# Reading the moving operand of fp32r products alternately from two halves of its block

## The chip, the cores and the metric

The kernel runs on one core of a Trainium2 chip. The metric is the device time of one execution in microseconds; the figure for the kernel before is the median of three runs. The profile comes from one more execution, and its span reaches from the first to the last instruction. The weights are permuted on the host before the launch; that is not part of the time.

## The reference

One layer of a hybrid encoder over 256 tokens with 2048 features, all in fp32. Cut to its products:

```python
mod = c_act @ ada_w + ada_b                     # 2048 x 12288: shift, scale, gate for two sub-layers
h = rms_norm(x, norm_mix_w) * (1 + scale_m) + shift_m
proj = h @ w_in                                 # q, k, v, o, z, conv inputs, gates, merge gates
h_a = bidirectional(mlstm_chunkwise, ...)       # 4 heads
y_a = (sigmoid(a_o) * rms_norm(h_a)) @ w_branch_a
qkv = silu(centred_depthwise_conv(b_qkv, gdn_conv_w))
o_b = bidirectional(gated_delta_chunkwise, ...) # 16 heads
y_b = (rms_norm(o_b) * silu(b_z)) @ w_branch_b
x = x + gate_m * ((g_a * y_a + g_b * y_b) @ w_out)
hf = rms_norm(x, norm_ffn_w) * (1 + scale_f) + shift_f
gt, up = split(hf @ w_gate_up)                  # 2048 x 11264
x = x + gate_f * ((silu(gt) * up) @ w_down)     # 5632 x 2048
return rms_norm(x, norm_final_w)
```

The change concerns all weight products except the modulation and the first sixteen column blocks of the input projection.

## The kernel before

**Split products.** A weight product is computed from fp32r operands, in three parts. Each operand is a high part (its rounding to fp32r) plus a low part (the remainder): `hh` and `hl` for the tokens, `wh` and `wl` for the weights. The product is high x high + low x high + high x low, added up in PSUM. TensorE takes a stationary operand of 128 x 128, loaded by an instruction of its own, and streams a moving operand of up to 512 columns past it.

**Two forms of product.** A product *by feature* (`fjob`, line 173) takes a block of 128 output features. The weight block `wh[:, k]` (128 x 128) is stationary and the tokens `hh[:, kk]` (256 columns) are the moving operand, in lines 187 to 189. The result has features on the partitions and tokens along the row. A product *by token* (`tjob`, line 195) takes 512 output features. The tokens `xh[:, kk, c]` (128 of them) are stationary and 512 weight columns are the moving operand, in lines 230 to 232; the result has tokens on the partitions. Where a product has `by_token`, its last chunk runs for one token block after the other (lines 253 to 255).

**Weights on their way.** The weights of one step come as a 1 MB block, issued by SyncE into one of three `raw` buffers. ScalarE copies half a block into `wh` (line 209 by token, 182 by feature), and VectorE subtracts to get `wl` (line 211 or 184). `wh` and `wl` have three buffers each; a buffer comes free when the last product that reads it is done. A block by token feeds 24 products. On the host, `_groups` (line 1449) and the array `gu` (line 1507) lay the weights out so that a block of 4 x 128 rows by 512 columns is one contiguous piece.

**Evictions.** A finished product by feature is copied out of PSUM by ScalarE: into a padded buffer for the convolution (`gdn_conv`, line 329, the `b` products) or into a buffer that goes to memory (`keep_f`, line 358, the `a` products). Products by token are read out by ScalarE or VectorE in `done` functions, in the order of their columns. There are four accumulators of one PSUM bank each (`acc_ps`).

**Order of the work.** The first part (line 557) works with full-precision fp32 products. Then the heads of the gated delta rule run between the projection products, which fill TensorE while the heads' short steps wait for each other (`fill`, `stream`). The mLSTM heads follow, then the branch and output projections. The feed-forward layer alternates a gate and an up product for each of eleven blocks of 512 features, then runs the down product in four groups of columns. Modulation sums on VectorE are spread over all of this (`pump`, `ada_parts`). The head steps include one in which 64 lanes invert 32 x 32 triangles by shrinking column loops (lines 692 and 698, on VectorE), the mLSTM's denominators (line 950), and the scores of a head (line 630), which are full-precision fp32 products.

Of the kernel before, what the change touches and what calls it, by code (L numbers as in the profile page):

```python
# [11 lines left out]
AF = mybir.ActivationFunctionType  # L12
# [3 lines left out]
P = 128  # L16
T = 256
D = 2048
KB = D // P
# [33 lines left out]
def hybrid_block(ctx: ExitStack, tc: tile.TileContext, xr, nfr, crow, pk_d, cst_d, ada2, ada4, win0, winb, wint, wba, wbb, wo, wgu, wd, out, dbg=None):  # L53
    nc = tc.nc
    V, S, G, PE = nc.vector, nc.scalar, nc.gpsimd, nc.tensor
# [12 lines left out]
    def big(p, dt, name):  # L68
        return p.tile([P, KB, T], dt, tag="b16", name=name)

    def order(ins, yes=True):

        return tc.keep_in_program_order(ins) if yes else ins
# [62 lines left out]
    def raw_tile(shape, name):  # L136

        since[0] += 1
        if since[0] > 2 and asked and room[0][0] is st:
            add()  # L140
        return st.tile(shape, F32, tag="raw", bufs=3, name=name)
# [4 lines left out]
    def settle(keep=0, only=None):  # L146

        now = [f for f in behind if only is None or f.__name__ == only]
        for f in now[: len(now) - keep]:
            behind.remove(f)  # L150
            f()
# [13 lines left out]
    def pump():  # L165
        count[0] += 1
        if every[0] and count[0] % every[0] == 0:
            owed[0] += 1
        if owed[0] and not held[0]:
            owed[0] -= 1  # L170
            sums()

    def fjob(name, src, done):

        ps = acc_ps.tile([P, 512], F32, tag="acc", name=f"acc_{name}")
        o = ps[:, :T]
        raw = raw_tile([P, KB, P], f"raw_{name}")
        nc.sync.dma_start(raw, src)
        for k0 in range(0, KB, 8):
            wh = st.tile([P, 8, P], F32R, tag="wh", bufs=3, name=f"wh_{name}_{k0}")  # L180
            wl = st.tile([P, 8, P], F32R, tag="wl", bufs=3, name=f"wl_{name}_{k0}")
            S.activation(wh, raw[:, k0 : k0 + 8], AF.Copy)
            settle()
            V.tensor_tensor(wl, raw[:, k0 : k0 + 8], wh.bitcast(F32), ALU.subtract)
            for k in range(8):
                kk = k0 + k
                PE.matmul(o, wh[:, k], hh[:, kk], start=kk == 0, stop=False)  # L187
                PE.matmul(o, wh[:, k], hl[:, kk], start=False, stop=False)  # L188
                PE.matmul(o, wl[:, k], hh[:, kk], start=False, stop=kk == KB - 1)  # L189
            if k0:  # L190
                pump()
                done(o)
            yield True

    def tjob(name, chunks, xh, xl, done, early=0, by_token=None, steps=1, parts=((0, slice(0, 512)), (1, slice(0, 512)))):

        raws = {}

        def halves(u, k0):
            if u not in raws:
                raws[u] = raw_tile([P, 4, 512], f"raw_{name}_{u}")
                nc.sync.dma_start(raws[u], chunks[u])
            wh = st.tile([P, 2, 512], F32R, tag="wh", bufs=3, name=f"wh_{name}_{u}_{k0}")
            wl = st.tile([P, 2, 512], F32R, tag="wl", bufs=3, name=f"wl_{name}_{u}_{k0}")
            order(S.activation(wh, raws[u][:, k0 : k0 + 2], AF.Copy), early)  # L209
            settle()  # L210
            order(V.tensor_tensor(wl, raws[u][:, k0 : k0 + 2], wh.bitcast(F32), ALU.subtract), early)  # L211
            return wh, wl

        todo = [(u, k0) for u in range(len(chunks)) for k0 in (0, 2)]
        made = []
        for i, q in enumerate(todo[:early]):
            made.append(halves(*q))
            if steps > 1 or i == early - 1:
                yield True
        ps = [acc_ps.tile([P, 512], F32, tag="acc", name=f"acc_{name}_{t}") for t in range(2)]  # L220
        last = 4 * len(chunks) - 1
        if by_token:
            todo = todo[:-2]
        for n, (u, k0) in enumerate(todo):
            wh, wl = made.pop(0) if made else halves(u, k0)
            for k in range(2):
                kk = 4 * u + k0 + k
                for t in range(2):
                    c = slice(t * P, (t + 1) * P)
                    order(PE.matmul(ps[t], xh[:, kk, c], wh[:, k], start=kk == 0, stop=False), early and steps > 1)  # L230
                    PE.matmul(ps[t], xl[:, kk, c], wh[:, k], start=False, stop=False)  # L231
                    PE.matmul(ps[t], xh[:, kk, c], wl[:, k], start=False, stop=kk == last)  # L232
            if k0:
                pump()
                if u == len(chunks) - 1:
                    done(ps)
            yield True
            if early and steps > 1:
                if n + early < len(todo):
                    made.append(halves(*todo[n + early]))  # L240
                yield True
        if by_token:
            w = [halves(len(chunks) - 1, k0) for k0 in (0, 2)]
            by_token()
            for i, (t, part) in enumerate(parts):
                if i > 1:
                    ps.append(acc_ps.tile([P, 512], F32, tag="acc", name=f"acc_{name}_{i}"))
                c = slice(t * P, (t + 1) * P)
                o = ps[i][:, : part.stop - part.start]
                for k in range(4):  # L250
                    kk = last - 3 + k
                    wh, wl = (a[:, k % 2, part] for a in w[k // 2])
                    PE.matmul(o, xh[:, kk, c], wh, start=i == 2 and not k, stop=False)
                    PE.matmul(o, xl[:, kk, c], wh, start=False, stop=False)
                    PE.matmul(o, xh[:, kk, c], wl, start=False, stop=kk == last)
                done(t, ps[i], part)
                yield True
# [34 lines left out]
    hh = big(bigA, F32R, "hh")  # L292
    hl = big(bigA, F32R, "hl")
# [9 lines left out]
    for i in range(NP_):  # L303
        pd = fr.tile([P, T + 4], F32, name=f"pad{i}")
# [5 lines left out]
    def decay_load(h):  # L310
        al = als[h] = fr.tile([P, 2, T + 8], F32, tag="al", bufs=2, name=f"al{h}")
        order(G.memset(al[:, :, 0:8], 0.0))
        order(G.dma_start(al[:, :, 8:], alpha_d[:, h].partition_broadcast(P)))

    def gdn_conv(h, j, ps):

        if j == 0:
            kq = fr.tile([P, 2, T], F32, tag="kq", bufs=2, name=f"kq{h}")
            vf = fr.tile([P, T], F32, tag="vf", bufs=2, name=f"vf{h}")
            parts[h] = (kq, vf)  # L320
            if h == 1:
                decay_load(h)
        kq, vf = parts[h]
        cb = (16 + h, h, 32 + h)[j]
        w = [pk[:, PK_CONV + 5 * cb + i : PK_CONV + 5 * cb + i + 1] for i in range(5)]
        pd = pads[npad[0] % NP_]
        npad[0] += 1
        if ps is not None:
            S.activation(pd[:, 2 : T + 2], ps, AF.Copy)
        settle(1)  # L330
        cv = fr.tile([P, T], F32, tag="cv", bufs=2, name=f"cv{h}_{j}")
        S.activation(cv, pd[:, 2 : T + 2], AF.Copy, scale=w[2])
        for i in (0, 1, 3, 4):
            V.scalar_tensor_tensor(cv, pd[:, i : i + T], w[i], cv, ALU.mult, ALU.add)

        def end():
            order(S.activation(kq[:, j] if j < 2 else vf, cv, AF.Silu))
            if ps is None:
                evict(3 * h + j + 1 + NP_)

        behind.append(end)
# [13 lines left out]
    def keep_f(dst, name):  # L355
        def done(ps):
            ev = evp.tile([P, T], F32, tag="evf", bufs=2, name=f"ev_{name}")
            S.activation(ev, ps, AF.Copy)
            S.dma_start(dst, ev)
        return done  # L360

# [29 lines left out]
    def evict(o):  # L391

        if o <= 3 * GRP:
            S.activation(pads[(o - 1) % NP_][:, 2 : T + 2], first[o], AF.Copy)
# [597 lines left out]
    last = (0, 1, 2, 1, 2, 2, 1, 1, 3, 0)  # L992
# [433 lines left out]
    for g in range(4):  # L1426
        c = slice(g * 512, (g + 1) * 512)
# [18 lines left out]
    return np.ascontiguousarray(w.reshape(kb, P, nb, P).transpose(2, 1, 0, 3))  # L1446


def _groups(w):
    k, n = w.shape  # L1450
    return np.ascontiguousarray(w.reshape(k // 512, 4, P, n // 512, 512).transpose(3, 0, 2, 1, 4))


def _fm(v):
# [3 lines left out]
def _arrays(x, c, ada_w, ada_b, norm_mix_w, w_in, mlstm_b_i, mlstm_b_f, mlstm_norm_w, gdn_conv_w,  # L1458
# [26 lines left out]
    w = w_in[0]  # L1485
# [5 lines left out]
    for h in range(NH_A):  # L1491
# [15 lines left out]
    gu = w_gate_up[0].reshape(4, 4, P, 2, KD, 512).transpose(4, 3, 0, 2, 1, 5)  # L1507
# [9 lines left out]
        "winb": np.ascontiguousarray(win[13:]),  # L1517
        "wint": wint,
        "wba": _groups(w_branch_a[0]),
        "wbb": _groups(w_branch_b[0]),  # L1520
        "wo": _groups(w_out[0]),
        "wgu": np.ascontiguousarray(gu),
        "wd": _groups(w_down[0]),
    }

# [16 lines left out]
```

## Time and profile before

| | us |
|---|---|
| runs: median (lowest to highest of 3) | 2053.01 (2051.42 to 2057.70) |
| the profiled execution: span | 2054.3 |
| TensorE with a product under way | 2017.2 |
| VectorE busy | 1397.7 |
| ScalarE busy | 1027.4 |
| mean granted TensorE clock | 0.992 |

In the profile, PE is the products on TensorE, PEld the loads of stationary operands (which run beside the products), DVE is VectorE, ACT ScalarE, POOL GpSimd and SP SyncE. A group's row gives the line of the kernel, the engine, the operation, the tile written and the tiles read, the shape and the count, then the busy time in us and the mean duration of one in ns, then the idle time before and what ended it. A product's duration counts from its start to the end of its drain, and the next product starts earlier than that.

### The profile page before, as it was taken

To read this page: it belongs to the slowest core of one execution; us is meant where nothing else is said; L and a number is where in the kernel's file an instruction comes from. 1 tells how busy PE (TensorE), PEld (TensorE's weight loads), DVE (VectorE), ACT (ScalarE), POOL (GpSimd) and SP (SyncE) were. 2 spreads that over 40 slices of the span, in tenths; PEclk is the share of its full clock that TensorE was granted. 3 is DMA by queue.
4 is the path that set the end of the run, shared out by engine and by line. 5 is a ranking of instruction groups with operands and counts; after the bars stand their busy time and mean duration, and the time that the engine had idled before them with its cause. 6 is when DMAs were issued, how large, how long until landed. Compare 5 with 4: busy or idle time off the path is not lost.

```text
span 2054.3 us, 27025 instructions
## 1 busy us (share of the span) xinstructions
PE 2017.2 (98%) x10386; PEld 1698.6 (83%) x10386; DVE 1397.7 (68%) x2062; ACT 1027.4 (50%) x1541; POOL 116.6 (6%) x211
## 2 busy tenths in 40 slices
PE   8999999999999999999999999999999999999998
PEld 6878789988997888889787888788888888878886
DVE  5778877877888788866577778756556554555554
ACT  3146647765675667455534444644444444444443
POOL 0001210111011010100100000200000000000000
PEclk9999999999999999999999999999999999999999
DMA  9986666656666666686776877466666665555553
GB/s 400 420 332 209 195 224 227 220 165 212 226 199 221 245 205 226 205 288 260 260 269 254 309 292 289 163 236 237 237 226 234 254 226 187 193 194 196 193 192 136
DMA packets 78962, 485.64 MB, mean 236 GB/s; under 512 B 10585, under 2 KB 15969, under 8 KB 24433
## 3 DMA queue, kind: packets, MB, share of 16 engines
q1 hardware_dynamic: 63216, 450.69, 60.5%
q0 software_dynamic: 8160, 17.88, 3.9%
q10 hardware_dynamic: 7458, 15.36, 2.0%
q8 instruction: 81, 1.33, 0.3%
q14 instruction: 47, 0.39, 0.1%
HBM read 467.07 MB, written 16.82 MB: 236 GB/s over the span
## 4 chain that ended last, share of the span: by engine, by line
PE 86%; DMA 6%; DVE 5%; ACT 1%; issue 1%; POOL 0%; ACTq 0%; SPq 0%; DVEq 0%; POOLq 0%
PE acc_gt L230 4%; PE acc_gt L232 4%; PE acc_gt L231 4%; PE acc_up L232 4%; PE acc_up L231 4%; PE acc_up L230 4%; PE acc_d L230 4%; PE acc_d L232 4%; PE acc_d L231 4%; DMA ra<-ada 3%; PE acc_o L232 3%; PE acc_o L230 3%; PE acc_o L231 3%; PE acc_b L187 2%; PE acc_b L188 2%; PE acc_b L189 2%
## 5 line engine op out<-in xcount | busy, mean ns | idle before, releaser
L211 DVE TENSOR_TENSOR wl_d<-raw_d,wh_d 128x1024 fp32r<-128x1024 f32 x88 | 107.9, 1226 | 119.9 <-ACT wh_d L209 119.9
L211 DVE TENSOR_TENSOR wl_up<-raw_up,wh_up 128x1024 fp32r<-128x1024 f32 x88 | 107.8, 1226 | 111.9 <-ACT wh_up L209 111.9
L211 DVE TENSOR_TENSOR wl_gt<-raw_gt,wh_gt 128x1024 fp32r<-128x1024 f32 x88 | 108.6, 1234 | 89.1 <-ACT wh_gt L209 89.1
L187 PE MATMUL acc_b<-hh,wh_b 128*128 128x256 f32 x576 | 164.7, 286 | 0.0
L209 ACT ACTIVATE wh_d<-raw_d 128x1024 fp32r<-128x1024 f32 x88 | 93.3, 1061 | 139.0 <-PE acc_d L231 134.0
L189 PE MATMUL acc_b<-hh,wl_b 128*128 128x256 f32 x576 | 160.8, 279 | 0.0
L188 PE MATMUL acc_b<-hl,wh_b 128*128 128x256 f32 x576 | 159.6, 277 | 0.0
L209 ACT ACTIVATE wh_gt<-raw_gt 128x1024 fp32r<-128x1024 f32 x88 | 93.3, 1060 | 128.7 <-PE acc_gt L231 77.3
L111 DVE SCALAR_TENSOR_TENSOR ada<-ada,crow 128x2048 f32<-128x2048 f32 x64 | 146.2, 2284 | 10.8 <-DMA ada<-ada 10.8
L209 ACT ACTIVATE wh_up<-raw_up 128x1024 fp32r<-128x1024 f32 x88 | 93.2, 1060 | 118.0 <-PE acc_up L231 84.2
L230 PE MATMUL acc_gt<-wh_gt,hfh 128*128 128x512 f32 x352 | 139.2, 395 | 0.1
L231 PE MATMUL acc_gt<-wh_gt,hfl 128*128 128x512 f32 x352 | 138.3, 393 | 0.0
L232 PE MATMUL acc_gt<-wl_gt,hfh 128*128 128x512 f32 x352 | 137.5, 391 | 0.0
L230 PE MATMUL acc_up<-wh_up,hfh 128*128 128x512 f32 x352 | 136.9, 389 | 0.0
L231 PE MATMUL acc_up<-wh_up,hfl 128*128 128x512 f32 x352 | 136.9, 389 | 0.0
L232 PE MATMUL acc_up<-wl_up,hfh 128*128 128x512 f32 x352 | 136.9, 389 | 0.0
L230 PE MATMUL acc_d<-wh_d,ffh 128*128 128x512 f32 x344 | 134.3, 391 | 0.0
L231 PE MATMUL acc_d<-wh_d,ffl 128*128 128x512 f32 x344 | 134.3, 390 | 0.0
L232 PE MATMUL acc_d<-wl_d,ffh 128*128 128x512 f32 x344 | 133.9, 389 | 0.0
L557 PE MATMUL first<-x,raw 128*128 128x256 f32 x512 | 115.9, 386 | 6.4 <-ACT x L551 6.4
L557 PEld LDWEIGHTS first<-x,raw 128*128 128x128 f32 x512 | 97.3, 192 | 25.1 <-ACT x L551 12.0
L187 PEld LDWEIGHTS acc_b<-hh,wh_b 128*128 128x128 f32 x576 | 108.4, 188 | 1.2 <-issue 0.9
(374 smaller groups left out, 5262.6 us busy)
## 6 DMA issues: line engine op xcount, KB each, us to landing
ada<-ada SPq DMA_DIRECT2D x64, 1024.0 KB, 4.9
raw_gt<-wgu SPq DMA_DIRECT2D x44, 1024.0 KB, 4.9
raw_up<-wgu SPq DMA_DIRECT2D x44, 1024.0 KB, 4.9
raw_d<-wd SPq DMA_DIRECT2D x44, 1024.0 KB, 4.8
raw_b<-winb SPq DMA_DIRECT2D x36, 1024.0 KB, 5.0
ra<-ada SPq DMA_DIRECT2D x32, 1025.0 KB, 15.3
raw<-win SPq DMA_DIRECT2D x16, 1024.0 KB, 14.5
raw_z<-wint SPq DMA_DIRECT2D x16, 1024.0 KB, 5.5
```

The lines of the kernel that those rows point to most:

```text
L111: order(V.scalar_tensor_tensor(raw, raw, 1.0, row_c[:, :D], ALU.mult, ALU.mult, accum_out=mod[:, c : c + 1]), room[0][3] > 1)
L187: PE.matmul(o, wh[:, k], hh[:, kk], start=kk == 0, stop=False)
L188: PE.matmul(o, wh[:, k], hl[:, kk], start=False, stop=False)
L189: PE.matmul(o, wl[:, k], hh[:, kk], start=False, stop=kk == KB - 1)
L209: order(S.activation(wh, raws[u][:, k0 : k0 + 2], AF.Copy), early)
L211: order(V.tensor_tensor(wl, raws[u][:, k0 : k0 + 2], wh.bitcast(F32), ALU.subtract), early)
L230: order(PE.matmul(ps[t], xh[:, kk, c], wh[:, k], start=kk == 0, stop=False), early and steps > 1)
L231: PE.matmul(ps[t], xl[:, kk, c], wh[:, k], start=False, stop=False)
L232: PE.matmul(ps[t], xh[:, kk, c], wl[:, k], start=False, stop=kk == last)
L557: PE.matmul(first[o], raw[:, o], x[:, b], start=b == 0 and o % 2 == 0, stop=b == KB - 1 and o % 2 == 1)
```

## The change

The moving operand of every fp32r product is read in another order. `woven` turns a row of n columns into pairs: first column 0 of the first half and column 0 of the second half, then column 1 of each, and so on. By token, the host stores each block of 512 weight columns so that this order gives the original columns one after the other (`_woven`): the even columns in the first half and the odd ones in the second. The results therefore stand in PSUM in the same places as before. By feature, the moving operand is the tokens, which are not permuted; their result stands in PSUM alternately from the two halves of the tokens, and the two ScalarE copies that read it out put it back in order by reading PSUM in steps of two columns. The stationary operands are read as before, and the splits work on the permuted weights as they did on the others.

```diff
@@ fjob
-                PE.matmul(o, wh[:, k], hh[:, kk], start=kk == 0, stop=False)
-                PE.matmul(o, wh[:, k], hl[:, kk], start=False, stop=False)
-                PE.matmul(o, wl[:, k], hh[:, kk], start=False, stop=kk == KB - 1)
+                PE.matmul(o, wh[:, k], woven(hh[:, kk]), start=kk == 0, stop=False)
+                PE.matmul(o, wh[:, k], woven(hl[:, kk]), start=False, stop=False)
+                PE.matmul(o, wl[:, k], woven(hh[:, kk]), start=False, stop=kk == KB - 1)
             if k0:
                 pump()
-                done(o)
+                done(o.rearrange("p (c h) -> p h c", h=2))
             yield True
+
+    def woven(a, n=2):
+
+        return a.rearrange("p (h c) -> p c h", h=n)
@@ tjob
-                    order(PE.matmul(ps[t], xh[:, kk, c], wh[:, k], start=kk == 0, stop=False), early and steps > 1)
-                    PE.matmul(ps[t], xl[:, kk, c], wh[:, k], start=False, stop=False)
-                    PE.matmul(ps[t], xh[:, kk, c], wl[:, k], start=False, stop=kk == last)
+                    order(PE.matmul(ps[t], xh[:, kk, c], woven(wh[:, k]), start=kk == 0, stop=False), early and steps > 1)
+                    PE.matmul(ps[t], xl[:, kk, c], woven(wh[:, k]), start=False, stop=False)
+                    PE.matmul(ps[t], xh[:, kk, c], woven(wl[:, k]), start=False, stop=kk == last)
...
-                    wh, wl = (a[:, k % 2, part] for a in w[k // 2])
+                    wh, wl = (woven(a[:, k % 2])[:, part.start // 2 : part.stop // 2] for a in w[k // 2])
@@ gdn_conv
-            S.activation(pd[:, 2 : T + 2], ps, AF.Copy)
+            S.activation(pd[:, 2 : T + 2].rearrange("p (h c) -> p h c", h=2), ps, AF.Copy)
@@ keep_f
-            S.activation(ev, ps, AF.Copy)
+            S.activation(ev.rearrange("p (h c) -> p h c", h=2), ps, AF.Copy)
@@ host
+def _woven(w, n=2):
+
+    return np.ascontiguousarray(w.reshape(*w.shape[:-1], -1, n).swapaxes(-1, -2)).reshape(w.shape)
+
+
 def _groups(w):
     k, n = w.shape
-    return np.ascontiguousarray(w.reshape(k // 512, 4, P, n // 512, 512).transpose(3, 0, 2, 1, 4))
+    return _woven(w.reshape(k // 512, 4, P, n // 512, 512).transpose(3, 0, 2, 1, 4))
...
-        "wgu": np.ascontiguousarray(gu),
+        "wgu": _woven(gu),
```

## The prediction

> **What bounds the kernel now.** I read the busy times and the slices first, then the chain of waits, then the timeline of TensorE at single products, because the change touches nothing else that is long.
>
> ```profile
> span 2054.3 us, 27025 instructions
> PE 2017.2 (98%) x10386; PEld 1698.6 (83%) x10386; DVE 1397.7 (68%) x2062; ACT 1027.4 (50%) x1541; POOL 116.6 (6%) x211
> PEclk9999999999999999999999999999999999999999
> PE 86%; DMA 6%; DVE 5%; ACT 1%; issue 1%; POOL 0%; ACTq 0%; SPq 0%; DVEq 0%; POOLq 0%
> L187 PE MATMUL acc_b<-hh,wh_b 128*128 128x256 f32 x576 | 164.7, 286 | 0.0
> L230 PE MATMUL acc_up<-wh_up,hfh 128*128 128x512 f32 x352 | 136.9, 389 | 0.0
> ```
>
> TensorE has work in 98% of the span at a full granted clock, and the chain lies on it for 86%. So the time is the number of products times the interval from one to the next. The mean of 389 ns in a row is no interval, since a product is still draining while the next one streams. The interval has to be read from the starts. Two stretches of the timeline (start, duration, both in us; first and last of 28 rows by token, and of 38 rows by feature):
>
> ```profile
> 1599.83 0.39 PE L230 MATMUL acc_gt<-wh_gt,hfh 128*128 128x512 f32 x1
> ...
> 1605.94 0.39 PE L230 MATMUL acc_up<-wh_up,hfh 128*128 128x512 f32 x1
> ```
>
> ```profile
> 399.80 0.28 PE L189 MATMUL acc_b<-hh,wl_b 128*128 128x256 f32 x1
> ...
> 403.99 0.28 PE L187 MATMUL acc_b<-hh,wh_b 128*128 128x256 f32 x1
> ```
>
> 27 intervals in 6.11 us are 226.3 ns for 512 moving columns; 37 intervals in 4.19 us are 113.2 ns for 256. Both are 0.442 ns per column, with nothing left over per instruction. Is that the array's own pace? The full-precision fp32 products say no:
>
> ```profile
> 239.76 3.43 PE ks L630 x8
> ```
>
> ```profile
> L630 PE MATMUL ks<-kq 128*128 128x512 f32 x64 | 30.3, 593 | 0.0
> ```
>
> Line 630 is reached 32 times (16 heads, two token blocks) and has 64 records, so each product is two instructions of 512 columns. Eight of them take 3.43 us of the chain: 428.8 ns each. I take that as two array passes per column, so 214.4 ns per pass of 512, which already holds the cost per instruction. The fp32r product has one pass and takes 226.3: **11.9 ns, 5.6%, are lost where the moving operand is read at one 4-byte column per pass**, and none where it is read at half that rate. That the place of the operands matters at all is seen in an earlier stage, with the same shape:
>
> ```profile
> 243.26 0.39 PE L231 MATMUL acc_v<-wh_v,hl 128*128 128x512 f32 x1
> ...
> 244.88 0.39 PE L232 MATMUL acc_v<-wl_v,hh 128*128 128x512 f32 x1
> ```
>
> Seven intervals in 1.62 us: 231.4 ns, 5.1 more than at 1600 us, with other tiles as operands.
>
> **The change part by part.** No product, load or split is added or removed. How many instructions read differently (windows over the whole span, of one line each: length, busy time and count):
>
> ```profile
> 0.00:2055.00 2055.00, 816.34 (x2064) 389.20 (x2064) 0.99 0.67 236
> ...
> 0.00:2055.00 2055.00, 224.49 (x784) 148.68 (x784) 0.99 0.67 236
> ...
> 0.00:2055.00 2055.00, 6.93 (x20) 3.79 (x20) 0.99 0.67 236
> ```
>
> These are lines 230, 187 and 253; each has two sister lines with the same count. By token: 3 x 2064, plus 12 of 512 columns in each of lines 253 to 255, make 6228. By feature: 3 x 784 = 2352. The 24 products of 256 columns in lines 253 to 255 are left out. Now they take 6228 x 0.2263 = 1409.4 us and 2352 x 0.1132 = 266.2 us.
>
> (a) *Products by token.* Each pair of neighbouring columns now comes from addresses 1024 bytes apart; each half is walked in order, one element every second column. No row of the trace shows such a moving operand, so I bound its cost. Below: a gain down to the pace of one fp32 pass, -11.9 ns each, -74.1 us. The reason for a gain at all is that each half alone is then read at 2 x 0.442 = 0.88 ns per element, about the pace of the fp32 rows (428.8 / 512 = 0.84 ns), which show no loss. Above: the only far jumps in the trace are VectorE's, in the inversion. At 264.7 us, 30 elements are 128 bytes apart (instruction one of line 698); at 298.0 us, the last one, 30 elements lie together:
>
> ```profile
> L698 DVE TENSOR_TENSOR uu<-uu,utmp x4: 203/225/261, 264.7 to 266.3; 64x30 f32<-64x30 f32 x1, 64x58 f32<-64x58 f32 x1, 64x84 f32<-64x84 f32 x1, 64x108 f32<-64x108 f32 x1
> ```
>
> ```profile
> L698 DVE TENSOR_TENSOR uu<-uu,utmp x6: 181/250/307, 293.1 to 298.0; 64x150 f32<-64x150 f32 x1, 64x130 f32<-64x130 f32 x1, 64x108 f32<-64x108 f32 x1, 64x84 f32<-64x84 f32 x1
> ```
>
> The shortest of each are the two: 203 against 181 ns, at most 0.73 ns a jump. At 512 jumps that is +375 ns a product, +2336 us, the far end. Between the ends I take the gain: the row nearest in kind is TensorE's own reading of fp32, and it says that the engine is free of the loss once an address stream runs at half pace. It doesn't say that two streams can run side by side; that is the main rival.
>
> [...]
>
> (b) *Products by feature.* Same reading, halves 512 bytes apart, but a second limit lies close by. Products with one moving column show what loading the stationary operand allows:
>
> ```profile
> 1063.42 2.74 PE L950 MATMUL pden<-ones,mdec 128*128 128x1 f32 x24
> 1066.02 0.48 PE L230 MATMUL acc_yb<-wh_yb,obh 128*128 128x512 f32 x1
> 1066.34 0.40 PE L231 MATMUL acc_yb<-wh_yb,obl 128*128 128x512 f32 x1
> ```
>
> The product issued at 1066.02 can have streamed from 1066.34 - 0.226 = 1066.11, so 24 loads took 2.69 us, 112 ns each. From 113.2 there are 1.2 ns to gain, 2.8 us in all.
>
> (c) *Evictions.* 49 ScalarE copies read PSUM in steps of two columns, 256 elements each.
>
> ```profile
> L329 ACT ACTIVATE pad<-acc_b 128x256 f32<-128x256 f32 x36 | 13.5, 374 | 2.9 <-PE acc_b L189 2.7
> L351 ACT ACTIVATE ev_mb<-acc_mb 128x512 f32<-128x512 f32 x8 | 4.8, 597 | 1.1 <-PE acc_mb L232 0.9
> 130.00:1000.00 870.00, 854.59 (x5235) 749.78 (x5235) 669.05 (x1276) 538.05 (x949) 96.33 (x183) 0.99 0.66 221
> ```
>
> From 256 to 512 elements a copy grows by 223 ns; if the step doubles that part, 49 x 0.223 = 11 us are added to ScalarE, which is busy 538 of 870 us in that stage, and four accumulators let TensorE run on. On the path: 0, and 11 us if that cover were gone. No gain is possible, since as many elements are read.
>
> (d) *Cover for a faster TensorE.* Per loaded block (24 products) it would need 24 x 0.2144 = 5.15 us instead of 5.43. In that time stand two splits on each of two engines and one load with three buffers:
>
> ```profile
> L209 ACT ACTIVATE wh_up<-raw_up 128x1024 fp32r<-128x1024 f32 x88 | 93.2, 1060 | 118.0 <-PE acc_up L231 84.2
> L211 DVE TENSOR_TENSOR wl_up<-raw_up,wh_up 128x1024 fp32r<-128x1024 f32 x88 | 107.8, 1226 | 111.9 <-ACT wh_up L209 111.9
> raw_up<-wgu SPq DMA_DIRECT2D x44, 1024.0 KB, 4.9
> ```
>
> 2.12 us of ScalarE, 2.45 us of VectorE, 4.9 us of load behind two more in flight: covered. Next to come late would be VectorE between 130 and 1000 us, 669 of 870 us busy beside conv, heads and the background sums. I allow 3 us there.
>
> Sum: 2054.3 - 74.1 - 2.8 + 3 = 1980.4 us of span. The median of the runs, 2053.0, is 1.3 below the profiled span, so 1979 for the runs.
>
> **The rivals.**
>
> *Half pace (slower).* The reader fetches neighbours together, and a column from a far address costs a fetch of its own. It decides from 0.442 ns per column upward, since products by token have no slack: each further 0.01 ns costs 6228 x 512 x 0.01 = 32 us. For it: the loss grows with the columns and not with the instructions, so the fetch is at its limit already, and breaking up neighbours can only ask more of it. Against it: nothing measured, only the reading of (a). Price: at the fp32 pace, 428.8 and 214.4 ns, it adds 6228 x 0.2025 + 2352 x 0.1012 = 1499 us, 3553 us in all; at exactly double, 1409.4 + 266.2 more, 3730 us. [...]
>
> *Worse placed (slower).* Two streams meet the weight load in the same part of the memory more often, and every product by token gets what those at 243 us have, +5.1 ns: 6228 x 0.0051 = +32 us, 2086 us. For it: that row; against it: the same row shows that most tiles are free of it.
>
> *No change.* The 5.6% belong to the fp32r format and not to reading; then the span stays at 2054 and the runs at 2053. Against it: 226.3 and 231.4 for one shape.
>
> **How the numbers follow.** Gain 0.45, half pace 0.34, worse placed 0.14, no change 0.07. The first is the likeliest single case, though the two slower ones together weigh about as much. Its own range is 1968 (the 231.4 of some 2300 early products vanish as well, 11 us more) to 2016 (half of the loss stays). The range has to hold the other cases: 1968 to 3740, where only the VectorE price (over 4000 us) lies outside. A measurement of this kernel tells about 0.3%, 6 us, from no change; so faster 0.45, same 0.07, slower 0.48.
>
> **What would show it.** Right: starts of neighbouring products on lines 230 to 232 lie 214 to 217 ns apart, those of lines 187 to 189 at 112 to 113, lines 329 and 358 may take up to 600 ns without TensorE waiting for an accumulator, and the splits wait as much for TensorE as now. Half pace: starts 430 to 453 ns apart by token, over 210 by feature, while VectorE and ScalarE fall to some 40 and 30% busy. Worse placed: 229 to 232 ns in all stages. The forecast is wrong if the intervals do not shrink, or if they do and the gaps before the products grow by as much.

## The result and the profile after

The changed kernel takes 1993.76 us (median of four runs, 1992.12 to 1999.19) against 2053.79 us for the kernel before beside it: a ratio of 0.9714, interval 0.9696 to 0.9733, 60 us less. The forecast was 1979.

The page of the changed kernel: span and instructions; busy times; the granted clock; the chain of waits by engine; the two groups shown of before. Its line numbers are higher by 4 behind `woven`.

```profile
span 1992.6 us, 27027 instructions
PE 1943.2 (98%) x10386; PEld 1700.4 (85%) x10386; DVE 1393.9 (70%) x2062; ACT 1023.7 (51%) x1541; POOL 116.8 (6%) x211
PEclk9999999999989999999999999999999999999999
PE 72%; DVE 12%; DMA 10%; ACT 3%; issue 2%; POOL 0%; ACTq 0%; SPq 0%; DVEq 0%; POOLq 0%
L187 PE MATMUL acc_b<-hh,wh_b 128*128 128x256 f32 x576 | 164.2, 285 | 0.0
L234 PE MATMUL acc_up<-wh_up,hfh 128*128 128x512 f32 x352 | 133.4, 379 | 0.0
```

The same work stands on the same engines; a product by token is 10 ns shorter. But the chain that was 86% on TensorE is 72% on it now: VectorE and DMA have come into it. The intervals, from the timeline (start and duration in us; first and last of 29 rows by token, of 7 by feature):

```profile
1549.63 0.38 PE L235 MATMUL acc_gt<-wh_gt,hfl 128*128 128x512 f32 x1
...
1555.67 0.38 PE L236 MATMUL acc_gt<-wl_gt,hfh 128*128 128x512 f32 x1
```

```profile
399.82 0.28 PE L189 MATMUL acc_b<-hh,wl_b 128*128 128x256 f32 x1
...
400.49 0.28 PE L189 MATMUL acc_b<-hh,wl_b 128*128 128x256 f32 x1
```

By token, 28 intervals in 6.04 us are 215.7 ns each (226.3 before). By feature, 6 in 0.67 us are 112 ns each (113.2 before).

**Where the rest went.** Both traces hold the same 10386 products in the same order, so every interval between two starts can be set beside the same interval of the other kernel. I cut both traces at the first product of the heads' filler work (`acc_z`), of the branch projections (`acc_yb`) and of the feed-forward layer (`acc_gt`), and end at the last product. An interval that is under 0.24 us in both kernels belongs to products that run back to back. What these intervals save is what the faster reading is worth; the remaining, longer intervals hold the waits.

| stage | length before, after (us) | saved | saved by back-to-back intervals | given back in longer intervals |
|---|---|---|---|---|
| heads | 873.8, 857.8 | 16.0 | 28.5 | 12.5 |
| branches and output | 295.7, 283.8 | 11.9 | 12.8 | 0.9 |
| feed-forward | 736.8, 703.0 | 33.8 | 34.4 | 0.6 |

The feed-forward stage keeps nearly all of it. The head stage gives nearly half of it back. Its windows (length, then busy time and count of each engine), first before, then after:

```profile
134.00:1009.00 875.00, 859.85 (x5245) 751.40 (x5245) 672.63 (x1277) 541.30 (x955) 98.56 (x187) 0.99 0.65 220
```

```profile
134.00:992.00 858.00, 831.96 (x5240) 746.88 (x5239) 671.47 (x1277) 538.33 (x952) 98.06 (x186) 0.99 0.67 224
```

TensorE without work: 15.2 us before, 26.0 after. What it waits for in that stage (total, times, longest), first before, then after:

```profile
PE vps L601 <- ACT vf L337: 4.0, 5, 2.5
PE acc_z L232 <- DVE wl_z L211: 3.0, 2, 2.0
...
PE acc_mb L232 <- DVE wl_mb L211: 1.3, 1, 1.3
...
PE acc_v L232 <- DVE wl_v L211: 0.8, 1, 0.8
...
PE acc_ma L232 <- DVE wl_ma L211: 0.4, 1, 0.4
```

```profile
PE vps L605 <- ACT vf L341: 6.3, 8, 3.1
PE acc_mb L236 <- DVE wl_mb L215: 3.1, 3, 1.5
...
PE acc_z L236 <- DVE wl_z L215: 2.4, 3, 1.5
PE acc_v L236 <- DVE wl_v L215: 2.4, 3, 1.4
PE acc_ma L236 <- DVE wl_ma L215: 2.1, 1, 2.1
PE p L762 <- DVE pt L754: 1.9, 1, 1.9
```

It is no single wait that grew, but many small ones: on the low part of the weights for products by token (`wl_mb`, `wl_v`, `wl_ma`), and on the heads' steps (`vps`, `p`).

### The profile page after: what moved, and what is told of

Same layout as the page of the kernel before. It is cut to its first block, busy times and chain, and to the rows that moved or that the text cites. A ratio compares the mean times of both kernels' runs of the same rounds, so it can differ in the third digit from the quotient of the medians.

```text
span 1992.6 us, 27027 instructions
## 1 busy us (share of the span) xinstructions
PE 1943.2 (98%) x10386; PEld 1700.4 (85%) x10386; DVE 1393.9 (70%) x2062; ACT 1023.7 (51%) x1541; POOL 116.8 (6%) x211
## 4 chain that ended last, share of the span: by engine, by line
PE 72%; DVE 12%; DMA 10%; ACT 3%; issue 2%; POOL 0%; ACTq 0%; SPq 0%; DVEq 0%; POOLq 0%
PE acc_gt L234 4%; PE acc_gt L235 4%; PE acc_gt L236 4%; PE acc_up L236 4%; PE acc_up L234 4%; PE acc_up L235 4%; PE acc_d L236 4%; PE acc_d L234 4%; PE acc_d L235 4%; DMA ra<-ada 3%; PE acc_o L236 2%; PE acc_o L234 2%; PE acc_o L235 2%; DMA ada<-ada 2%; PE acc_ya L236 1%
## 5 line engine op out<-in xcount | busy, mean ns | idle before, releaser
L111 DVE SCALAR_TENSOR_TENSOR ada<-ada,crow 128x2048 f32<-128x2048 f32 x64 | 146.2, 2284 | 12.7 <-DMA ada<-ada 12.5
L189 PEld LDWEIGHTS acc_b<-hh,wl_b 128*128 128x128 f32 x576 | 111.3, 193 | 1.2 <-DVE wl_b L184 1.1
```

What stands on the lines that cost most here:

```text
L111: order(V.scalar_tensor_tensor(raw, raw, 1.0, row_c[:, :D], ALU.mult, ALU.mult, accum_out=mod[:, c : c + 1]), room[0][3] > 1)
L189: PE.matmul(o, wl[:, k], woven(hh[:, kk]), start=False, stop=kk == KB - 1)
```

## The experiments

### One form of product alone

```diff
@@ token_only: fjob, gdn_conv, keep_f as before the change
-                PE.matmul(o, wh[:, k], woven(hh[:, kk]), start=kk == 0, stop=False)
+                PE.matmul(o, wh[:, k], hh[:, kk], start=kk == 0, stop=False)
...
-                done(o.rearrange("p (c h) -> p h c", h=2))
+                done(o)
@@ feature_only: tjob, _groups, wgu as before the change
...
-                    PE.matmul(ps[t], xl[:, kk, c], woven(wh[:, k]), start=False, stop=False)
+                    PE.matmul(ps[t], xl[:, kk, c], wh[:, k], start=False, stop=False)
...
-    return _woven(w.reshape(k // 512, 4, P, n // 512, 512).transpose(3, 0, 2, 1, 4))
+    return np.ascontiguousarray(w.reshape(k // 512, 4, P, n // 512, 512).transpose(3, 0, 2, 1, 4))
```

> Only the products by token are woven; products by feature and their two ScalarE copies are as before. If the parts add up by the intervals (by token 11 to 13 ns less per product, by feature held by the weight load near 112 ns), this takes 1996 to 1999 us, and products by feature start 113.2 ns apart. The rival, that the copies in steps of two columns cost time on the path, expects it below the whole change, 1985 to 1992 us.

> Only the products by feature are woven, with the two copies in steps of two columns. By the intervals 2352 x 1.2 to 1.7 ns = 3 to 4 us are gained: 2049 to 2051 us, products by feature 112 ns apart, products by token 226 to 232 ns as before. If the copies cost time, 2054 us or more.

By token alone: 1996.11 us, ratio 0.9718 (0.9696 to 0.9739). By feature alone: 2048.54 us, ratio 0.9981 (0.9969 to 0.9993). That is 57.7 and 5.3 us, 63.0 together, where both at once give 60.0: the parts add up within the intervals. Paired with the kernel before, the back-to-back intervals of the products that are woven save 71.1 us by token and 7.8 by feature; in the changed kernel the two kinds save 71.0 and 5.2. The rival of the first run, that the copies in steps of two columns cost time on the path, expected 1985 to 1992 us and is not borne out: the changed kernel's line 333 has a median of 368 ns (line 329 before: 367), and the version with these copies, by feature, is the one that gains. By feature more is gained than the 2.8 us that I had worked out, though the interval of the run (1.4 to 6.4 us) holds 2.8 too. In the traces, one in ten of the plain products by feature starts 118 ns or more after the one before it, where the woven ones have 112 at that rank.

### Which order of reading is free

Two kernels give each kind of product by token an order of its own, with the weights laid out on the host to match.

```diff
+    def weave(a, key):
+
+        h, c = WEAVES[key]
+        if h == 1:
+            return a
+        if h * c == 512:
+            return a.rearrange("p (h c) -> p c h", h=h)
+        return a.rearrange("p (b h c) -> p b c h", h=h, c=c)
...
-                    PE.matmul(ps[t], xl[:, kk, c], woven(wh[:, k]), start=False, stop=False)
+                    PE.matmul(ps[t], xl[:, kk, c], weave(wh[:, k], key), start=False, stop=False)
@@ dist_b adds two orders
+        if WEAVES[key] == "lanes":
+            return a.rearrange("p h (b f) -> p b f h", f=4)[:, :, 2 * k : 2 * k + 2]
+        a = a[:, k]
+        if WEAVES[key] == "pairs":
+            return a.rearrange("p (h b c) -> p b h c", h=2, c=2)
```

> Products by feature as in the changed kernel. Products by token each with a pattern of their own; the distance in bytes between the two neighbours of a pair: gate 8, up 16, down 32, branch a 64, branch b 128, z 256, v 512, w_out 1024 (as in the change); merge a in four quarters of 512 bytes; merge b as one stream in steps of 8 bytes (twice through the block), output gate as one stream in steps of 16 bytes (four times through). [...] Theory 2, the two neighbours must lie in different regions of the memory: only far distances (512 bytes and more) give 216, the near ones 226 to 232. Theory 3, any order that does not take neighbouring addresses one after the other avoids the loss: all patterns, the single streams too, give 216. Whole kernel 1985 to 2055 us, by how many of them lose.

> Second set of orders for products by token, each told by its interval. [...] Up: two columns from the first half, two from the second, in turn. Branch a: eight streams 256 bytes apart, branch b: sixteen streams 128 bytes apart, merge a: four streams 16 bytes apart, output gate: four streams 512 bytes apart, merge b: one stream in steps of 32 bytes; z as before the change; down, v and w_out as in the change. [...] Theory D (distance): four streams 16 bytes apart are faster than four 512 bytes apart. z 226 to 232, down, v and w_out 216 under all.

The instructions of single tiles in the first kernel (durations in ns: shortest, median, longest; then the first and last start):

```profile
L246 PE MATMUL acc_gt<-wh_gt,hfh x352: 389/389/797, 1471.4 to 1932.2; 128*128 128x512 f32 x176
L246 PE MATMUL acc_up<-wh_up,hfh x352: 378/379/379, 1496.8 to 1952.9; 128*128 128x512 f32 x176
L246 PE MATMUL acc_v<-wh_v,hh x128: 379/379/780, 161.1 to 259.1; 128*128 128x512 f32 x128
L246 PE MATMUL acc_ma<-wh_ma,hh x128: 436/442/833, 352.7 to 1188.1; 128*128 128x512 f32 x128
L246 PE MATMUL acc_mb<-wh_mb,hh x128: 614/644/697, 259.7 to 1062.0; 128*128 128x512 f32 x128
L246 PE MATMUL acc_o<-wh_o,hh x128: 621/644/808, 303.2 to 1114.6; 128*128 128x512 f32 x128
```

And in the second:

```profile
L251 PE MATMUL acc_gt<-wh_gt,hfh x352: 387/389/792, 1579.6 to 2158.7; 128*128 128x512 f32 x176
L251 PE MATMUL acc_up<-wh_up,hfh x352: 496/513/513, 1605.4 to 2191.0; 128*128 128x512 f32 x176
L251 PE MATMUL acc_ya<-wh_ya,hah x128: 685/689/1052, 1297.5 to 1489.1; 128*128 128x512 f32 x128
L251 PE MATMUL acc_yb<-wh_yb,obh x128: 603/627/995, 1110.1 to 1296.2; 128*128 128x512 f32 x128
L251 PE MATMUL acc_ma<-wh_ma,hh x128: 430/436/829, 332.9 to 1109.3; 128*128 128x512 f32 x128
L251 PE MATMUL acc_mb<-wh_mb,hh x128: 590/607/670, 259.3 to 1002.0; 128*128 128x512 f32 x128
```

A duration holds the drain too: in the changed kernel a product by token lasts 0.38 us and the next one starts 215.7 ns after it. What a product costs is the interval between starts; its medians, worked out from the same traces, are:

| order of the 512 columns | interval, ns |
|---|---|
| plain, one column after the other | 227 (229 in the head stage) |
| two streams, 8 bytes apart | 227 |
| two streams, 16, 32, 64, 128, 256, 512 or 1024 bytes apart | 216 each |
| two streams 2048 bytes apart, each taking two neighbouring columns and leaving out the next two | 227 |
| two columns of one half, two of the other | 340 |
| four streams, 16 bytes apart | 269 |
| four streams, 512 bytes apart | 279 |
| eight streams; sixteen streams | 487; 435 |
| one stream in steps of 8, 16, 32 bytes | 453, 460, 431 |

The whole kernels take 2198 and 2437 us, one run each; the first was expected at 1985 to 2055, because I had not reckoned with single streams and quarters as slow as these.

Theory 2 (far regions) falls: 16 bytes are as good as 1024, 216 ns each. Theory 3 (any scattered order) falls: steps of one stream take 431 to 460 ns, about double the plain 227. The reason given in the prediction, two streams at half pace, holds for two streams from 16 bytes on (216); at 8 bytes they keep the plain order's 227.

The second kernel narrows it. Its gate products take their columns in turn from two blocks 2048 bytes apart, and each of the two streams takes two neighbouring columns, leaves out the next two and goes on (these products mix two weight blocks, so the output is not the layer's). They get 227. At 8 bytes apart, too, a stream takes two neighbouring columns and leaves out two: 227. At 16 bytes apart it takes four in a row, at 1024 bytes 256: 216. So it takes no nearness of the two streams to lose the 11 ns; what goes with the loss, among the orders in which two streams take turns column by column, is that each leaves its place after two columns. One difference is left: 2048 bytes with four columns in a row was not run, though all distances from 16 to 1024 bytes give the same 216.

The other orders cost more. Two columns of one half and two of the other, in turn, take 340, and eight streams (487) more than any single stream in steps (460 at most). Four streams take 269 at 16 bytes and 279 at 512; the sign is that of theory D, distance, by 10 ns. Why two columns in a row lose what four do not, and what happens in the orders that are slower still, these runs do not show.

### What gives the gain back in the head stage

First the order of the low part, where TensorE was seen to wait:

```diff
@@ low_last: in tjob, for the half block
...
-                    PE.matmul(ps[t], xh[:, kk, c], woven(wl[:, k]), start=False, stop=kk == last)
...
+            for k, t in every_kt:
+                kk, c = 4 * u + k0 + k, slice(t * P, (t + 1) * P)
+                PE.matmul(ps[t], xh[:, kk, c], woven(wl[:, k]), start=False, stop=kk == last)
```

> The changed kernel, with the order of the 12 products of a half block changed: all eight with the high part of the weights first, then the four with the low part. In the changed kernel TensorE waits 11.4 us for the low part (VectorE), all at the first product that reads it. If the lost part of the gain sits in that wait, the low part gets six products, 1.3 us, more time and the kernel takes 1982 to 1989 us. If the splits are bound by throughput in those places, the wait moves to the next high part and the time stays at 1991 to 1995 us.

1991.78 us, ratio 0.9705 (0.9682 to 0.9728): the same as the change within the interval, as expected if the wait only moves. The waits of products by token on `wl` fell from 11.4 us to 5.3, and others grew (in the profiled execution, over the span):

```profile
PE vps L606 <- ACT vf L342: 7.8, 6, 3.1
...
PE p L754 <- DVE R L723: 5.2, 2, 3.8
PE acc_v L237 <- DVE wl_v L215: 4.6, 2, 3.9
```

Here the wait only moved; its place is not its cause. One stage, the first branch projection, was shorter by 2.6 us in that execution (105.7 to 103.1), so I tried the order in the two branch projections alone, with the change itself for comparison:

> The changed kernel once more, to see how far its time and the waits of its head stage differ between executions: 1992 to 1999 us, head stage 854 to 860 us.

> The changed kernel with the low part of the weights last in the two branch projections alone, where the kernel with that order everywhere needed 103.1 us for the first of them and the changed kernel 105.7. If that gain stands by itself: 2 to 3 us below the changed kernel of the same call. The rival, that it was chance of one execution: no difference.

1993.06 us (ratio 0.9708, 0.9693 to 0.9724) for the change and 1998.09 us (0.9722, 0.9699 to 0.9745) for the other: no gain, and none of these versions beats the change. The head stage of the change took 852.6 us in this execution (854 to 860 were expected) and 857.8 in the first, so single executions differ there by 5 us.

Then two loads were taken from VectorE. Without two convolution taps:

```diff
@@ taps_before, taps_after
-        for i in (0, 1, 3, 4):
+        for i in (1, 3):
```

> The kernel before with two of the four VectorE taps of each convolution left out: 96 instructions of 0.48 us, 46 us of VectorE, all between 130 and 810 us. In the kernel before the chain of that stage lies on TensorE, so both theories expect little: 2045 to 2054 us.

> The same two taps left out of the changed kernel. By its intervals the change should save some 75 to 80 us, and 60 are measured; in the head stage (134 to 992 us) TensorE is idle 26 us where it was 15 before. If VectorE, 78% busy there, holds the rest back, the saving against the kernel before with the same taps left out grows to 66 to 76 us (1974 to 1984 us). If the heads' round trips between engines hold it back whatever VectorE has to do, the saving stays at 58 to 63 us.

2047.71 us (0.9983, 0.9973 to 0.9992) and 1986.0 us (0.9668, 0.9646 to 0.9690): 61.7 us between them, as much as with all taps. 46 us less for VectorE do not bring the lost gain back, where 66 to 76 us were expected if VectorE's load held it. Without the modulation sums:

```diff
@@ noada_before, noada_after
-    background.append(ada_parts(2, 3, 4))
+    V.memset(mod[:, 2 * KB : 5 * KB], 0.5)
```

> The kernel before without the 48 modulation sums of parts 2 to 4 and their 1 MB loads (a constant stands in their place), which run between the heads and hold one of the three buffers for weight blocks. The chain of the kernel before lies on TensorE, so little is gained: 2035 to 2051 us.

> The changed kernel without the same sums and loads. Theory B: in the head stage a weight block has to wait for a buffer, land (5 us) and be split (2.3 us) while a product by feature takes 5.4 us of TensorE, and the sums leave two of three buffers for it; that holds the rest of the gain back. Then the saving against the kernel before without the sums is 70 to 80 us, against 60 with them, and TensorE's long waits in the head stage are alike in the two (within 5 us). Theory R: the heads' own round trips between engines hold it back; then the saving stays at 58 to 66 us and the long waits differ by 10 us or more.

2038.26 us (0.9918, 0.9894 to 0.9942) and 1973.25 us (0.9602, 0.9582 to 0.9623): 65.0 us between them, a ratio of 0.968 against 0.971 with the sums, which the intervals do not separate. The long waits seem to say more. Intervals over 0.5 us in the head stage, less 0.25 us each, add up as follows:

| | kernel before | changed kernel |
|---|---|---|
| as they are | 19.9 | 31.1 (28.8 in the second execution) |
| without two taps | 13.6 | 27.0 |
| without the modulation sums | 13.1 | 16.8 |

With the sums the change lengthens the long waits by 9 to 11 us (13 with two taps left out), without them by 4, as theory B has it. But the 13.1 us hold one wait of the mLSTM heads that no other of these kernels has at that length:

```profile
PE ph L966 <- ACT hs L968: 3.9, 1, 3.9
```

Without the intervals before `ph` products the growth is 9.4 us without the sums (6.2 to 15.6), against 10 to 12 with them. Interval by interval, the longer intervals of the head stage grow as follows (us, kernel with the change less the same kernel without it; the products by whose start an interval ends):

| | by token | by feature | `ph` | other heads' products | sum |
|---|---|---|---|---|---|
| as they are | 6.7 | 0.2 | -0.4 | 6.0 | 12.5 |
| as they are, second execution | 5.2 | 0.5 | -0.4 | 4.1 | 9.5 |
| only products by token woven | 4.4 | 0.5 | -0.4 | 0.9 | 5.4 |
| only products by feature woven | -5.2 | 0.1 | 1.1 | 2.5 | -1.4 |
| without two taps | 7.1 | 1.1 | 2.2 | 6.7 | 17.1 |
| without the modulation sums | 6.8 | 0.8 | -5.3 | 3.1 | 5.5 |

Wherever products by token are woven, these intervals before them grow by 4 to 7 us, with the sums or without. (That they shrink by 5.2 where only products by feature are woven shows how far single executions spread.) So the two kernels without sums do not show that the sums hold the gain back: what looked like it is mostly the one wait of `ph`.

Theory B also started from the round trip of a weight block by feature. A stretch of the chain in the changed kernel shows it: a block is issued once a `raw` buffer is free, lands, is copied, and is subtracted, and a modulation sum comes soon after on VectorE:

```profile
499.12 1.24 DVE wl_b L184
...
500.38 4.77 DMA raw_b<-winb
...
505.25 1.07 ACT wh_b L182
...
506.34 1.23 DVE wl_b L184
...
511.13 2.20 DVE ada L111
```

From the end of one split to the end of the next lie 7.2 us, for a block that TensorE uses up in 48 x 0.112 = 5.4 us. But before the change it was 48 x 0.1132 = 5.4 us as well, and products by feature wait at most 1 us more than before. This round trip can't be what the change made worse.

Theory R, the heads' own round trips between engines, gets the time right (65.0 us, in its 58 to 66), and the long waits nearly so once `ph` is left out (9.4 us apart, where it expected 10 or more). Theory B gets the long waits only as first added up, and not the time. But R does not explain the part that goes back before products by token, which wait on the low part of the weights from VectorE. So the traces show where the gain goes back, and the cause stays open: steps of the heads that have less time of filler products to hide behind, and the order of VectorE's work, were not separated.

## Why the prediction was right

*What bounds the kernel*: right. The time was products times interval, and shortening the interval shortened the kernel.

*The direction* was the likeliest single case and not a safe one: 0.45 for faster against 0.48 for slower. As the prediction says, no row showed that two streams can be read side by side, so that they can was a choice that came out well. The stated range, up to 3740 us, hardly tested it. What did test it is the interval: 214 to 217 ns were named as the sign, and 215.7 came.

*(a) By token*: right in size. 74.1 us were worked out; the back-to-back intervals of these products save 71.0. The interval came to 215.7 and not 214.4 ns. The 214.4 came from halving an fp32 instruction, and with it any cost per instruction. If that instruction is two passes in 428.8 ns and the woven product one in 215.7, such a cost is 2 x 215.7 - 428.8 = 2.6 ns, an estimate; how many passes either of them is, no run shows. The prediction read that nothing is left over per instruction, because 256 and 512 columns gave the same 0.442 ns per column. The woven products do not keep that: 112 ns for 256 columns are 0.44 per column, 215.7 for 512 are 0.42. What the longer interval lost came back in part in the head stage, where products by token fell to the same 216 from 229.

*The reason given*, two streams at half pace: borne out for two streams, by the distances from 16 bytes up (216 ns), and narrower than I put it: each stream took four columns or more in a row, and with two in a row it is 227. That a stream has a pace of its own is still an inference, since more than two streams (269 to 487) do not follow it.

*(b) By feature*: right in kind, 2.8 us worked out, 5.3 measured (5.2 in the intervals of the changed kernel). They stop at 112 ns, the pace at which the prediction's 24 loads followed each other, but the plain ones were slower on the mean (117.6 ns over all short intervals) than the stretch at 400 us that I took.

*(c) Evictions*: right, and free for a better reason than cover: the copy takes no more time than before (368 against 367 ns).

*(d) Cover*: **the step that was mis-sized.** I allowed 3 us; the head stage gives back 12.5 (9.5 in the second execution). It is the largest part of what the forecast missed: 75 us were expected and 60 came. I compared what the engines have to do per block, and such totals don't show when a wait ends. The place was named rightly, between 130 and 1000 us, and waits on VectorE's splits did grow there, but the heads' own steps came late as well, and 46 us less work for VectorE did not bring the gain back. Why these waits grow stays open.

*Half pace*, the main rival: it exists, as 431 to 460 ns for a single stream in steps, but not in the order that the change uses: there neighbours by token come from addresses 1024 bytes apart, and a product takes 216 ns. That far columns cost a fetch of their own was a supposition, and no run shows single fetches. *Worse placed*: the reverse came, woven products take 216 ns in every stage. *No change*: out.

## What to carry to other kernels

Where a moving operand of 4-byte columns sets the pace, read the intervals between starts and compare them with a form that reads more slowly. In this kernel 11 of the 227 ns of a product of 512 columns were in the order of reading, and they were had back (216) by taking neighbours from two places 16 to 1024 bytes apart, with at least four columns in a row from each. Steps (431 to 460 ns), four streams or more (269 to 487), and pairs from one place (340) cost much more than they could bring.

When TensorE gets faster, set the two traces side by side, product by product: the intervals that stay short show what the change is worth, the long ones where it is given back. And before a sum of waits is put down to a cause, look whether one long wait makes it up, in the kernel before too.

## What the runs showed of the hardware

Plain fp32r products of 512 columns started 226 to 232 ns apart. In a stretch of `acc_z` products, from 141 to 146 us of the kernel before, those of lines 231, 232 and 230 took 226, 229 and 231 to 232 in turn; what decides it was not tested. The woven ones of 512 columns took 216 in every stage. Two streams 8 bytes apart keep the loss (227), 16 bytes lose it (216). Steps of 16 bytes in one stream (460) and two streams 1024 bytes apart (216) both leave the neighbourhood with every column and differ by more than a factor of two, so the jump alone does not make the difference. ScalarE read PSUM in steps of two columns at the pace of neighbouring ones (368 against 367 ns for 256 elements).
